# Lead of weight sums, order of block products and deferred token sums in the FFN of a four-layer decoder

## The chip, the cores and the metric

The kernel runs on one core of a Trainium2 chip. The metric is the device time of one execution, in microseconds (us); three runs of the kernel before took 2438.58 to 2440.51 us, median 2439.3. TensorE (PE) multiplies, VectorE (DVE), ScalarE (ACT) and GpSimd (POOL) work element by element, SyncE (SP) issues DMAs. POOL issues DMAs too, and only through its queue are the accumulating ones issued.

## The reference

512 tokens of width 1024 go through four layers in float32. Each layer adds a token mixer (0 and 3: gated linear recurrence "lru"; 1: sparse attention "nsa"; 2: gated linear attention "gla") and then a SwiGLU channel mixer (FFN) of inner width 2816; a last norm follows.

```python
def swiglu(h, w_gate, w_up, w_down):
    return (jax.nn.silu(h @ w_gate) * (h @ w_up)) @ w_down
...
        h = h + y
        h = h + swiglu(rmsnorm(h, ffn_norm[layer]), ffn_w_gate[layer], ffn_w_up[layer], ffn_w_down[layer])
    return rmsnorm(h, final_norm)
```

## The kernel before

**Precision.** Every float32 operand is split into a high part (`hi`, an ACT copy to the short float type) and a low part (`lo`, a DVE subtraction); a product is three matmuls, hi by hi, hi by lo and lo by hi.

**The FFN** of a layer runs in three thirds (8, 8 and 6 tiles of 128 of the inner width), each in two units (4 and 4, 4 and 4, 3 and 3 tiles) and a down projection (`project`, tiles `pj`). So a layer has six units, and the first one directly follows the mixer's output projection. A unit (L551 on) computes gate and up together for its tiles by seven block products in place of eight: `b11`, `t1`, `b22`, `t2`, `t3`, `b21`, `t4`. Each is a `step` (L528): two token halves, four k tiles, three matmuls, so 24 matmuls of 128 columns of tokens by 512 (or 384) of weights. The operands are sums: on the token side a11, a12, a22 and s1 to s4, on the weight side the blocks of gate (b11, b21) and up (b12, b22) for the first and second half of the width, and their sums `t1` = b12+b11, `t2` = b12+b11+b22, `t3` = b12+b22 and `t4` = b12+b11+b22+b21. Steps add up in the PSUM banks X, Z and Y; ACT and DVE copy and combine these between steps (`a`, `z` and the others), so X can hold several products one after another.

**Token sums.** `project` adds each finished bank to h (L494) and calls `finalize` (L423) for it, this calls `combine` (L400): for k under 4 it makes a11 (`ph`, `pl`) and s3; for k from 4 on it makes, in one go, `xf` (h times gain), s1 and s2 (tile `s`, halves `sh`, `sl`), the parts of x (`xh`, `xl`: a12 and a22) and s4. Then `finalize` adds the square (`sq`) for the norm. `norm_sum` (L448), some matmuls `nsum`, a DVE row `ms` and a POOL row `rstd`, comes three steps after the unit's start (`later(3)`).

**Weights.** All weights lie in `wall`, blocks of 512 KB. `uses` (L157) makes one list of them in the order in which PE takes them, with how each is made: plain (one load by SP, L236, into `raws`, tiles `wr`), first (load and one accumulating DMA on POOL's queue, L238, into `big`, tiles `wc`), sum (the same in `raws`), on (an accumulating DMA, L263, onto a tile that was used and split already: `t2` onto the tile of `t1`, `t4` onto that of `t2`). `take` (L270) is called as a step takes its weights: it keeps splits three uses ahead (ACT L258, DVE L259, into a ring of four `ws` tiles), loads five ahead, and in the FFN eight ahead. A load and its adds are issued together.

**What sets the order.** Within an engine rows are queued in the order of the program, as the scheduler of the framework has laid them out; a row that waits holds all rows behind it. So on POOL's queue an add that waits for its load holds later adds and POOL's own arithmetic. The engines run against each other by semaphores.

```python
        tt(s[:, a], x1[:, b], x[:, b], op=OP.subtract)
        tt(s[:, b], s[:, a], x1[:, a], op=OP.subtract)
        sh, sl = self.slot("sh", F32R), self.slot("sl", F32R)
        parts(s, sh, sl)
```

Of the kernel before, what the change touches and what calls it, by code (L numbers as in the profile page):

```python
# [8 lines left out]
F32 = mybir.dt.float32  # L9
F32R = mybir.dt.float32r  # L10
# [174 lines left out]
class Kernel:  # L185
    def __init__(self, tc, ctx, wall, xT, prm, cst, hot, relb, nsm, gsm, out, phases):
# [9 lines left out]
        self.lead.tile([128, pad // 4], F32, name="lead")  # L196
        self.raws = pool("raws", bufs=5)
# [3 lines left out]
        self.slots = pool("slots", bufs=56)  # L201
# [4 lines left out]
        self.raw, self.w = {}, {}  # L206
        self.now = 0
# [14 lines left out]

    RAW_AHEAD, SUM_AHEAD, SPLIT_AHEAD = 5, 8, 3

    def prefetch(self, upto):
        while self.n_dma < min(upto, len(self.uses)):
            i = self.n_dma
            how, blocks = self.uses[i][1:]
            self.n_dma += 1
            if how == "on":  # L230
                continue
            if how == "first":
                r = self.large([128, 1152], "wc")[:, 0:1024]
            else:
                r = self.raws.tile([128, 1024], F32, name=self.name("wr"), tag="wr")
            self.nc.sync.dma_start(r, self.wall[blocks[0]])  # L236
            for b in blocks[1:]:
                self.nc.gpsimd.dma_start(r, self.wall[b], accum_op=OP.add)  # L238
            self.raw[i] = r
# [138 lines left out]
    def new_norm(self, idx):  # L378
# [4 lines left out]
        if idx % 2:  # L383
            self.op = {n: {} for n in ("a11", "a12", "a22", "s1", "s2", "s3", "s4")}

    def gain(self, k):
        return self.prm[:, C_GAIN + self.gidx * 8 + k:C_GAIN + self.gidx * 8 + k + 1]

    def combine(self, k):
# [26 lines left out]
        xh, xl = self.slot("xh", F32R), self.slot("xl", F32R)  # L416
        parts(x, xh, xl)
        if k % 2 == 0:
            self.s4 = self.slot("s4h", F32R), self.slot("s4l", F32R)
        half = (a, b)[k % 2]  # L420
        tt(x[:, a], x[:, a], s[:, b], op=OP.add)
        parts(x[:, a], self.s4[0][:, half], self.s4[1][:, half])
        self.op["a12"][k], self.op["a22"][k] = (xh[:, a], xl[:, a]), (xh[:, b], xl[:, b])  # L423
        self.op["s1"][k], self.op["s2"][k] = (sh[:, a], sl[:, a]), (sh[:, b], sl[:, b])
        self.op["s4"][k] = self.s4[0][:, half], self.s4[1][:, half]

    def finalize(self, k, tk=slice(0, 512)):
# [8 lines left out]
        sq = self.slot("sq")  # L436
        nc.scalar.activation(sq[:, tk], h, AF.Square)
# [89 lines left out]

    def step(self, what, unit, banks, first, last):  # L528
# [17 lines left out]
    def unit(self, l, f, nf, waiting):  # L546
# [9 lines left out]
        for i in self.step("b11", u, X, True, False):
            copy(a1[i], X[i])
        while waiting:
            waiting.pop(0)()
        Z = [self.bank("Z") for _ in range(2)]  # L560
        for i in self.step("t1", u, Z, True, False):
            copy(z1[i], Z[i])
        for i in self.step("b22", u, Z, False, True):
            pass
        for i in self.step("t2", u, X, False, False):
            copy(a2[i], X[i])
            tt(a2[i], Z[i][:, 0:n], a2[i], op=OP.subtract)
        for i in self.step("t3", u, X, False, False):
            tt(z1[i], z1[i], X[i][:, 0:n], op=OP.subtract)
        Y = [self.bank("Y") for _ in range(2)]  # L570
        for i in self.step("b21", u, Y, True, True):
            tt(a1[i], Y[i][:, 0:n], a1[i], op=OP.add)
            silu(a1[i], a1[i], i)
            stt(a2[i], a2[i], self.rstd[:, i:i + 1], a1[i], op0=OP.mult, op1=OP.mult)
# [822 lines left out]
```

## Time and profile before

| | |
|---|---|
| median of three runs | 2439.3 us |
| profiled execution | 2447.19 us |
| its span | 2445.5 us |
| mean granted TensorE clock | 0.975 |
| PE busy | 2327.0 us, 95% |
| DVE / ACT / POOL busy | 60% / 50% / 17% |
| DMA queue q1 (SP) | 250.66 MB, 30.3% of 16 engines |
| DMA queue q0 (POOL) | 100.68 MB, 23.4% of 16 engines |

The span is what the trace covers; the execution's own time is a little longer. A timeline row gives start, duration, engine, line, operation, output and inputs, and in brackets how long the engine had idled just before and what ended that. [...]

### The profile page before, as it was taken

Reading aid. Unit: us, or ns where it says so; the run is one execution under the profiler, and the core shown is the slowest. Engines: PE = TensorE matmul, PEld = TensorE weight load, DVE = VectorE, ACT = ScalarE, POOL = GpSimd, SP = SyncE. Lnnn points to the kernel's source line nnn. Section 1 sums busy time; section 2 is a strip of 40 time slices with the busy share of each in tenths; the row PEclk is TensorE's granted clock in tenths of the full one; section 3 lists DMA queues with packets and bytes.
Section 4 is the critical chain, followed back from the end, with each engine's and each line's share of the span. In section 5 each row is a group of like instructions: output and inputs, shape, how many; then the busy total and the mean of one; then the engine's idle time right before and its main releaser. Section 6 shows DMA issues by size and latency. Waiting matters only on the chain.

```text
span 2445.5 us, 29511 instructions
## 1 busy us (share of the span) xinstructions
PE 2327.0 (95%) x10898; PEld 1941.3 (79%) x10898; DVE 1469.7 (60%) x2388; ACT 1224.6 (50%) x1963; POOL 418.3 (17%) x445
## 2 busy tenths in 40 slices
PE   8997999999999999999989998999989998899998
PEld 7876787887786777887978886788888877788787
DVE  7775546456269987555456536545455886555545
ACT  5954535343368766444445335535344774434344
POOL 1411101001157531010100000101010230101010
PEclk9998999999999999999999998999999999899999
DMA  7235858673421136676862214768684324668682
GB/s 249 86 101 124 207 146 218 157 193 91 143 81 27 44 87 161 184 185 185 207 180 97 82 61 112 183 163 208 170 232 139 104 71 131 152 172 190 175 195 87
DMA packets 102912, 353.21 MB, mean 144 GB/s; under 512 B 11632, under 2 KB 18416, under 8 KB 102768
## 3 DMA queue, kind: packets, MB, share of 16 engines
q1 hardware_dynamic: 75120, 250.66, 30.3%
q0 software_dynamic: 27648, 100.68, 23.4%
q8 instruction: 85, 1.39, 0.2%
q14 instruction: 59, 0.48, 0.1%
HBM read 346.04 MB, written 5.24 MB: 144 GB/s over the span
## 4 chain that ended last, share of the span: by engine, by line
PE 73%; DMA 9%; DVE 8%; ACT 6%; issue 2%; POOL 1%; POOLq 0%; SPq 0%; ACTq 0%; DVEq 0%
PE pj L301 9%; PE pj L302 9%; PE pj L300 9%; DMA wc<-wall 5%; PE X L541 5%; PE X L540 5%; PE X L542 5%; DMA wr<-wall 3%; PE Z L540 2%; PE Z L542 2%; PE Z L541 2%; PE lp L302 2%; PE lp L300 2%; PE lp L301 2%; DVE ws L259 2%
## 5 line engine op out<-in xcount | busy, mean ns | idle before, releaser
L259 DVE TENSOR_TENSOR ws<-wr,ws 128x1024 fp32r<-128x1024 f32 (+1 forms) x402 | 475.5, 1186 | 453.8 <-ACT ws L258 446.4
L258 ACT ACTIVATE ws<-wr 128x1024 fp32r<-128x1024 f32 (+1 forms) x402 | 408.4, 1020 | 466.6 <-PE pj L302 180.7
L259 DVE TENSOR_TENSOR ws<-wc,ws 128x1024 fp32r<-128x1024 f32 (+1 forms) x144 | 163.5, 1135 | 234.4 <-ACT ws L258 233.6
L258 ACT ACTIVATE ws<-wc 128x1024 fp32r<-128x1024 f32 (+1 forms) x144 | 142.2, 988 | 281.5 <-DMA wc<-wall 95.1
L301 PE MATMUL pj<-al,ws 128*128 128x512 f32 (+1 forms) x728 | 278.7, 383 | 0.0
L300 PE MATMUL pj<-ah,ws 128*128 128x512 f32 (+1 forms) x728 | 278.7, 384 | 0.0
L302 PE MATMUL pj<-ah,ws 128*128 128x512 f32 (+1 forms) x728 | 278.4, 382 | 0.0
L238 POOL DMA_DIRECT2D wr<-wall x48 | 42.0, 874 | 696.1 <-DMA wr<-wall 583.2
L263 POOL DMA_DIRECT2D wc<-wall x96 | 87.6, 998 | 421.4 <-DVE ws L259 394.9
L301 PEld LDWEIGHTS pj<-al,ws 128*128 128x128 f32 x728 | 136.9, 188 | 27.1 <-DVE al L329 1.1
L302 PEld LDWEIGHTS pj<-ah,ws 128*128 128x128 f32 x728 | 136.8, 188 | 26.4
L300 PEld LDWEIGHTS pj<-ah,ws 128*128 128x128 f32 x728 | 136.8, 188 | 26.2
L542 PE MATMUL X<-ws,pl 128*128 128x512 f32 (+1 forms) x384 | 142.5, 371 | 0.0
L540 PE MATMUL X<-ws,ph 128*128 128x512 f32 (+1 forms) x384 | 142.4, 371 | 0.0
L541 PE MATMUL X<-ws,ph 128*128 128x512 f32 (+1 forms) x384 | 142.4, 371 | 0.0
L302 PE MATMUL lp<-xh,ws 128*128 128x512 f32 x320 | 126.8, 398 | 10.0 <-DVE ws L259 10.0
L300 PE MATMUL lp<-xh,ws 128*128 128x512 f32 x320 | 127.2, 398 | 6.8 <-ACT ws L258 6.8
L301 PE MATMUL lp<-xl,ws 128*128 128x512 f32 x320 | 126.5, 395 | 0.0
L540 PE MATMUL Z<-ws,sh 128*128 128x512 f32 (+1 forms) x192 | 78.5, 409 | 35.9 <-ACT sh L396 35.9
L540 PE MATMUL Z<-ws,s4h 128*128 128x512 f32 (+1 forms) x192 | 79.4, 414 | 34.5 <-ACT z L552 34.5
L986 POOL TENSOR_TENSOR L<-L,sw 128x512 f32<-128x512 f32 (+3 forms) x128 | 90.9, 750 | 70.8 <-DVE lc L977 25.2
L494 DVE TENSOR_TENSOR h<-h,pj 128x512 f32<-128x512 f32 x116 | 77.5, 684 | 36.1 <-PE pj L302 36.1
(375 smaller groups left out, 5551.6 us busy)
## 6 DMA issues: line engine op xcount, KB each, us to landing
wr<-wall SPq DMA_DIRECT2D x410, 512.0 KB, 4.4
wc<-wall POOLq DMA_DIRECT2D x144, 512.0 KB, 6.8
wc<-wall SPq DMA_DIRECT2D x48, 512.0 KB, 4.3
wr<-wall POOLq DMA_DIRECT2D x48, 512.0 KB, 6.4
scr<-rb SPq DMA_DIRECT2D x16, 192.0 KB, 1.9
h<-xT SPq DMA_DIRECT2D x8, 256.0 KB, 5.7
bias<-scr SPq DMA_DIRECT2D x16, 128.0 KB, 2.7
out<-hg SPq DMA_DIRECT2D x16, 128.0 KB, 1.8
```

Source lines behind the costliest of these rows:

```text
L238: self.nc.gpsimd.dma_start(r, self.wall[b], accum_op=OP.add)
L258: self.nc.scalar.activation(hi, r, AF.Copy)
L259: self.nc.vector.tensor_tensor(lo, r, hi.bitcast(F32), op=OP.subtract)
L263: self.nc.gpsimd.dma_start(whole, self.wall[self.uses[on][2][0]], accum_op=OP.add)
L300: mm(ps, lhsT=wh, rhs=x[0], start=first, stop=False)
L301: mm(ps, lhsT=wh, rhs=x[1], start=False, stop=False)
L302: mm(ps, lhsT=wl, rhs=x[0], start=False, stop=last)
L494: nc.vector.tensor_tensor(self.h[m + c], self.h[m + c], banks[c], op=OP.add)
L540: mm(o, lhsT=xh, rhs=wh, start=first and k == 0, stop=False, skip_group_check=True)
L541: mm(o, lhsT=xh, rhs=wl, start=False, stop=False, skip_group_check=True)
L542: mm(o, lhsT=xl, rhs=wh, start=False, stop=k == 3, skip_group_check=True)
L986: nc.gpsimd.tensor_tensor(p, p, ww.to_broadcast([128, 128 * (i + 1)]), op=OP.mult)
```

## The change

Three things change. (1) The first unit of each FFN (f = 0) takes its products in the order b11, t3, t1, t2, b22, b21, t4 and its `t2` weights are a sum of their own (three blocks in a tile of their own); all other units take t1, b11, b22, t2, t3, b21, t4. (2) Loads and adds are issued apart: sums (first and sum) are loaded up to ten uses ahead, added up to seven; `raws` has six tiles for five, `slots` 54 for 56. (3) `combine` makes s1 at once and puts s2, s4, the parts of x and the squares off to the steps b11, t3, t1 and t2; `norm_sum` runs at the first unit's t2.

```diff
+def unit_order(key):
+    if key[2] == 0:
+        return "b11", "t3", "t1", "t2", "b22", "b21", "t4"
+    return "t1", "b11", "b22", "t2", "t3", "b21", "t4"
...
+                           "t2": ("first", ("b12", "b11", "b22")) if key[2] == 0 else ("on", ("b22",)),
...
-    RAW_AHEAD, SUM_AHEAD, SPLIT_AHEAD = 5, 8, 3
+    RAW_AHEAD, SUM_AHEAD, ADD_AHEAD, SPLIT_AHEAD = 5, 10, 7, 3
+
+    def load(self, i):
+        if i in self.raw or self.uses[i][1] == "on":
+            return
+        how, blocks = self.uses[i][1:]
+        if how == "first":
+            r = self.large([128, 1152], "wc")[:, 0:1024]
+        else:
+            r = self.raws.tile([128, 1024], F32, name=self.name("wr"), tag="wr")
+        self.nc.sync.dma_start(r, self.wall[blocks[0]])
+        self.raw[i] = r
+        if blocks[1:]:
+            self.adds[i] = blocks[1:]
+
+    def add(self, i):
+        for b in self.adds.pop(i, ()):
+            self.nc.gpsimd.dma_start(self.raw[i], self.wall[b], accum_op=OP.add)
...
+    def ahead(self, i):
+
+        self.prefetch(i + self.RAW_AHEAD)
+        for j in range(self.n_dma, min(i + self.SUM_AHEAD, len(self.uses))):
+            if self.uses[j][1] in ("first", "sum"):
+                self.load(j)
+        for j in range(i, min(i + self.ADD_AHEAD, len(self.uses))):
+            self.add(j)
...
             self.prefetch(i + 1)
+            self.add(i)
...
-        self.prefetch(i + 1 + self.RAW_AHEAD)
-        while self.n_dma < min(i + 1 + self.SUM_AHEAD, len(self.uses)) and self.keys[self.n_dma][0][0] in "bt":
-            self.prefetch(self.n_dma + 1)
+        self.ahead(i + 1)
...
         tt(s[:, a], x1[:, b], x[:, b], op=OP.subtract)
-        tt(s[:, b], s[:, a], x1[:, a], op=OP.subtract)
-        sh, sl = self.slot("sh", F32R), self.slot("sl", F32R)
-        parts(s, sh, sl)
...
+        parts(s[:, a], sh[:, a], sl[:, a])
...
+        def second():
+            tt(s[:, b], s[:, a], x1[:, a], op=OP.subtract)
+            parts(s[:, b], sh[:, b], sl[:, b])
...
+        for n, f in (("s2", second), ("s4", fourth), ("x", plain)):
+            self.waits[n].append(f)
...
+        for f in self.waits.pop({"b11": "s2", "t3": "s4", "t1": "x", "t2": "sq"}.get(what), ()):
+            f()
+        if what == "t2" and unit[1] == 0:
+            self.norm_sum()
...
+            elif what == "t2" and first:
+                tt(a2[i], a2[i], X[i][:, 0:n], op=OP.subtract)
+                tt(z1[i], z1[i], X[i][:, 0:n], op=OP.subtract)
...
+            elif what == "t3" and first:
+                tt(a2[i], X[i][:, 0:n], a1[i], op=OP.subtract)
...
+            elif what == "b22" and first:
+                tt(a2[i], Z[i][:, 0:n], a2[i], op=OP.add)
...
-        self.later(3, self.norm_sum)
```

The counts: PE has as many matmuls as before; DVE has 27 rows more, ACT some 8 more, SP 8 loads more and POOL 8 adds more over the kernel. Three places of the queues follow; line numbers of the changed kernel are its own, and banks are named there after the step that opens them (`b11` is the former X, `t1` the former Z).

PE in the first unit of layer 0, before: the last of `b11` has run, and `t1` (Z) begins; `ws_299` is the first of its two weight tiles, `sh` and `sl` its token sums.

```order
L540 MATMUL Z_346_1769<-ws_299_1583,sh_302_1605 128x512
L541 MATMUL Z_346_1769<-ws_299_1583,sh_302_1605 128x512
L542 MATMUL Z_346_1769<-ws_299_1583,sl_303_1606 128x512
L540 MATMUL Z_347_1770<-ws_299_1583,sh_302_1605 128x512
L541 MATMUL Z_347_1770<-ws_299_1583,sh_302_1605 128x512
L542 MATMUL Z_347_1770<-ws_299_1583,sl_303_1606 128x512
L540 MATMUL Z_346_1769<-ws_299_1583,sh_311_1639 128x512
L541 MATMUL Z_346_1769<-ws_299_1583,sh_311_1639 128x512
L540 MATMUL Z_347_1770<-ws_299_1583,sh_311_1639 128x512
L541 MATMUL Z_347_1770<-ws_299_1583,sh_311_1639 128x512
```

The same place after the change, from `b11`'s last row on; `ws_329` and `ws_334` are the two `t1` weight tiles.

```order
L586 MATMUL b11_327_1688<-ws_300_1585,pl_285_1477 128x512
L584 MATMUL t1_337_1786<-ws_329_1706,sh_304_1610 128x512
L584 MATMUL t1_338_1787<-ws_329_1706,sh_304_1610 128x512
L585 MATMUL t1_337_1786<-ws_329_1706,sh_304_1610 128x512
L586 MATMUL t1_337_1786<-ws_329_1706,sl_305_1611 128x512
L584 MATMUL t1_337_1786<-ws_329_1706,sh_308_1631 128x512
L585 MATMUL t1_337_1786<-ws_329_1706,sh_308_1631 128x512
L586 MATMUL t1_337_1786<-ws_329_1706,sl_309_1632 128x512
L584 MATMUL t1_337_1786<-ws_334_1751,sh_312_1652 128x512
L585 MATMUL t1_338_1787<-ws_329_1706,sh_304_1610 128x512
```

And a few rows on, still in the first unit after the change, where `t1`'s last rows with `ws_334` meet the first of `t3` (`ws_301`, onto the bank of `b11`, with the `ph` of k below 4).

```order
L584 MATMUL t1_337_1786<-ws_334_1751,sh_316_1673 128x512
L585 MATMUL t1_337_1786<-ws_334_1751,sh_316_1673 128x512
L586 MATMUL t1_337_1786<-ws_334_1751,sl_317_1674 128x512
L584 MATMUL b11_326_1687<-ws_301_1589,ph_269_1435 128x512
L585 MATMUL b11_326_1687<-ws_301_1589,ph_269_1435 128x512
L586 MATMUL b11_326_1687<-ws_301_1589,pl_270_1436 128x512
```

`t1` still comes first on PE, though the program has `t3` ahead of it; 21 of its 24 rows stand before `t3`, and the halves alternate in another way.

POOL's queue from the first to the second unit of layer 0, before: L238 is the add issued beside a load, L263 the add onto a used tile (`wc_362` and `wc_364`, the second unit's `t1`, twice: for `t2`, then for `t4`).

```order
L455 TENSOR_TENSOR rstd_356_1846<-ms_355_1844,mhalf_91 128x4
L238 DMA wr_384_2015<-wall 128x1024
L238 DMA wc_446_2411<-wall 128x1024
L238 DMA wc_448_2441<-wall 128x1024
L238 DMA wr_386_2021<-wall 128x1024
L263 DMA wc_362_1889<-wall 128x1024
L263 DMA wc_364_1895<-wall 128x1024
L263 DMA wc_362_1889<-wall 128x1024
L263 DMA wc_364_1895<-wall 128x1024
L238 DMA wc_486_2753<-wall 128x1024
```

After the change: L247 is the add beside or behind a load, L287 the add onto a used tile; `wc_349` and `wc_352` are the second unit's `t1`, `wr_372` and `wr_375` its `t3`, `wc_297` and `wc_299` the first unit's `t2`.

```order
L287 DMA wc_299_1558<-wall 128x1024
L247 DMA wr_372_1983<-wall 128x1024
L247 DMA wr_375_1990<-wall 128x1024
L495 TENSOR_TENSOR rstd_359_1864<-ms_358_1862,mhalf_91 128x4
L247 DMA wc_422_2287<-wall 128x1024
L247 DMA wc_425_2294<-wall 128x1024
L287 DMA wc_349_1810<-wall 128x1024
L287 DMA wc_352_1817<-wall 128x1024
L287 DMA wc_349_1810<-wall 128x1024
L287 DMA wc_352_1817<-wall 128x1024
```

The second unit's `t3` adds stood among the `wc` adds, directly ahead of `t2`'s; now they stand ahead of `rstd`, before both adds of the following third's first sums.

POOL's queue in the NSA mixer, before: scalings of the attention weights `L`, then the low parts of the keys (`kl`).

```order
L986 TENSOR_TENSOR L_912_5347<-L_912_5347,sw_951_5474 128x128 x4
L901 TENSOR_TENSOR kl_938_5439<-kw_821_4897,kh_937_5438 64x512
L902 TENSOR_TENSOR kl_938_5439<-kw_821_4897,kh_937_5438 64x512
L912 TENSOR_TENSOR qq_958_5505<-qw_763_4621,qq_958_5505 64x512
L912 TENSOR_TENSOR qq_959_5508<-qw_763_4621,qq_959_5508 64x512
```

After the change:

```order
L1046 TENSOR_TENSOR L_914_5363<-L_914_5363,sw_953_5490 128x128 x4
L247 DMA wr_1389_7010<-wall 128x1024
L961 TENSOR_TENSOR kl_940_5455<-kw_823_4913,kh_939_5454 64x512
L962 TENSOR_TENSOR kl_940_5455<-kw_823_4913,kh_939_5454 64x512
L972 TENSOR_TENSOR qq_960_5521<-qw_765_4637,qq_960_5521 64x512
L972 TENSOR_TENSOR qq_961_5524<-qw_765_4637,qq_961_5524 64x512
```

The add of a `t3` sum of the following FFN now stands between the scalings and `kl`.

## Rows read from the trace of the kernel before

**Rows 1.** The page, busy time by engine: busy us, share of the span, instructions.

```profile
PE 2327.0 (95%) x10898; PEld 1941.3 (79%) x10898; DVE 1469.7 (60%) x2388; ACT 1224.6 (50%) x1963; POOL 418.3 (17%) x445
```

**Rows 2.** Waits of PE by what it waited for: us in total, times, longest us.

```profile
PE Z L540 <- ACT sh L396: 35.9, 12, 4.8
PE Z L540 <- ACT z L552: 34.5, 12, 7.4
```

**Rows 3.** Windows over two stretches of 192 gate/up matmuls without a wait (a unit and the first step of the next), tiles of 512 and of 384 columns. The columns: window, its length, busy us of PE, weight loads, DVE, ACT and POOL (with instructions), granted clock, DMA share, GB/s.

```profile
345.90:389.43 43.53, 43.53 (x194) 35.99 (x192) 25.73 (x28) 23.50 (x27) 5.28 (x7) 1.00 0.78 197
471.50:504.77 33.27, 33.27 (x193) 33.24 (x192) 20.22 (x27) 18.80 (x27) 4.17 (x6) 1.00 0.76 199
```

**Rows 4.** Windows over the first unit of each FFN, layers 0 to 3, from the first matmul of `b11` to the end of `t4`; columns as in rows 3.

```profile
195.20:253.77 58.57, 46.08 (x177) 35.98 (x176) 36.85 (x54) 31.22 (x44) 6.26 (x7) 0.83 0.51 120
918.60:968.03 49.43, 43.33 (x177) 33.78 (x176) 35.02 (x51) 30.16 (x43) 6.48 (x6) 0.93 0.62 144
1501.26:1559.36 58.10, 45.61 (x177) 35.62 (x176) 37.03 (x54) 30.16 (x43) 6.33 (x7) 0.82 0.56 131
2060.08:2120.90 60.82, 48.33 (x177) 37.72 (x176) 36.86 (x54) 31.21 (x44) 6.26 (x7) 0.80 0.47 116
```

**Rows 5.** Timeline of PE in the first unit of layer 0: one of the waits in `t1`, two matmuls after it, and the matmuls of the norm.

```profile
211.97 0.80 PE L540 MATMUL Z<-ws,sh 128*128 128x512 f32 x1 [4.80 <-ACT sh L396]
...
212.99 0.63 PE L542 MATMUL Z<-ws,sl 128*128 128x512 f32 x1
213.42 0.63 PE L540 MATMUL Z<-ws,sh 128*128 128x512 f32 x1
...
223.34 0.83 PE L451 MATMUL nsum<-ones,sq 128*128 128x1 f32 x6
```

**Rows 6.** Timeline of ACT at the start of the same unit.

```profile
194.04 1.06 ACT L258 ACTIVATE ws<-wc 128x1024 fp32r<-128x1024 f32 x1 [8.46 <-PE pj L302]
195.00 0.70 ACT L400 ACTIVATE xf<-h,prm 128x512 f32<-128x512 f32 x1
...
197.66 0.64 ACT L396 ACTIVATE sh<-s 128x512 fp32r<-128x512 f32 x1 [1.00 <-DVE s L413]
...
216.24 0.63 ACT L396 ACTIVATE sh<-s 128x512 fp32r<-128x512 f32 x1 [0.95 <-DVE s L413]
```

**Rows 7.** Windows over the second unit of the thirds with 4 and 4 tiles, eight in all, from the first matmul of `t1` to the first of the down projection: two of them, and the sum of the eight. Columns as in rows 3.

```profile
391.09:426.17 35.08, 33.04 (x147) 27.04 (x146) 21.23 (x25) 17.74 (x22) 4.36 (x6) 1.00 0.87 215
...
2255.04:2290.05 35.01, 33.31 (x148) 26.96 (x146) 21.15 (x25) 17.74 (x22) 3.91 (x5) 1.00 0.87 214
sum 285.16, PE 270.83 PEld 219.87 DVE 169.67 ACT 142.05 POOL 31.72; mean PE 33.85 PEld 27.48 DVE 21.21 ACT 17.76 POOL 3.96
```

**Rows 8.** The same for the second units of the thirds with 3 and 3 tiles, layers 0 to 3.

```profile
506.00:535.61 29.61, 25.91 (x147) 25.03 (x146) 17.16 (x23) 14.43 (x22) 2.44 (x3) 1.00 0.83 203
1215.81:1250.34 34.53, 27.59 (x148) 27.27 (x147) 17.34 (x23) 14.66 (x22) 6.32 (x9) 0.90 0.89 227
1805.26:1840.52 35.26, 27.88 (x147) 27.55 (x146) 17.34 (x23) 14.65 (x22) 4.24 (x6) 0.85 0.87 221
2369.88:2399.07 29.19, 25.90 (x148) 25.00 (x146) 17.16 (x23) 14.43 (x22) 1.84 (x3) 1.00 0.81 206
```

**Rows 9.** Timelines of POOL (three rows), ACT (two) and PE (one) around the second unit of layer 0.

```profile
245.54 0.92 POOL L238 DMA_DIRECT2D wr<-wall  x1 [19.62 <-DMA wr<-wall]
...
260.06 0.86 POOL L238 DMA_DIRECT2D wr<-wall  x1 [4.37 <-DMA wr<-wall]
260.60 2.11 POOL L263 DMA_DIRECT2D wc<-wall  x2
...
272.29 1.06 ACT L258 ACTIVATE ws<-wc 128x1024 fp32r<-128x1024 f32 x1 [7.79 <-DMA wc<-wall]
273.25 0.58 ACT L552 ACTIVATE z<-Z 128x512 f32<-128x512 f32 x1
...
273.89 0.79 PE L540 MATMUL Z<-ws,s4h 128*128 128x512 f32 x1 [4.58 <-ACT z L552]
```

**Rows 10.** The page, groups of instructions: line, engine, operation, tiles, count, busy us, mean ns of one, idle before.

```profile
L259 DVE TENSOR_TENSOR ws<-wc,ws 128x1024 fp32r<-128x1024 f32 (+1 forms) x144 | 163.5, 1135 | 234.4 <-ACT ws L258 233.6
```

**Rows 11.** The page, DMA queues (packets, MB, share of 16 engines over the span), and DMA issues (count, KB each, median us from issue to landing).

```profile
q1 hardware_dynamic: 75120, 250.66, 30.3%
q0 software_dynamic: 27648, 100.68, 23.4%
...
wr<-wall SPq DMA_DIRECT2D x410, 512.0 KB, 4.4
wc<-wall POOLq DMA_DIRECT2D x144, 512.0 KB, 6.8
```

**Rows 12.** Windows in layer 2 ahead of the second unit of three tiles: the middle of the projection before that third, and the end of the third's first unit. Columns as in rows 3.

```profile
1745.00:1770.00 25.00, 25.00 (x112) 20.71 (x111) 9.07 (x11) 3.61 (x4) 2.60 (x3) 1.00 0.55 131
1788.00:1805.00 17.00, 17.00 (x103) 16.96 (x102) 12.41 (x18) 10.19 (x16) 3.91 (x6) 1.00 0.94 286
```

**Rows 13.** Timelines of SP (one row) and POOL (two) in the NSA mixer.

```profile
722.30 0.33 SPq L236 DMA_DIRECT2D wr<-wall  x1
...
723.69 1.28 POOL L901 TENSOR_TENSOR kl<-kw,kh 64x512 fp32r<-64x512 f32 x1
...
753.09 1.04 POOL L986 TENSOR_TENSOR L<-L,sw 128x512 f32<-128x512 f32 x1 [6.04 <-DVE lc L977]
```

More of the change, by code (lines that the diff above doesn't have):

```diff
@@ L170, in uses @@
         wall = lambda b, k: at[(b,) + unit + (k,)]
-        for step, how, blocks in (("b11", "plain", ("b11",)), ("t1", "first", ("b12", "b11")), ("b22", "plain", ("b22",)),
-                                  ("t2", "on", ("b22",)), ("t3", "sum", ("b12", "b22")), ("b21", "plain", ("b21",)),
-                                  ("t4", "on", ("b21",))):
+        for step in unit_order(key):
+            how, blocks = {"b11": ("plain", ("b11",)), "t1": ("first", ("b12", "b11")), "b22": ("plain", ("b22",)),
+                           "t2": ("first", ("b12", "b11", "b22")) if key[2] == 0 else ("on", ("b22",)),
+                           "t3": ("sum", ("b12", "b22")), "b21": ("plain", ("b21",)), "t4": ("on", ("b21",))}[step]
             for k in (0, 2):
@@ L205, in __init__ @@
         self.pos = self.n_dma = self.n_split = 0
-        self.raw, self.w = {}, {}
+        self.raw, self.w, self.adds = {}, {}, {}
         self.now = 0
@@ L227, in prefetch @@
             i = self.n_dma
-            how, blocks = self.uses[i][1:]
             self.n_dma += 1
[L230 to L239, printed above, removed]
+            self.load(i)
+    def ahead(self, i):
[5 more added lines that the diff above has]
+            self.add(j)
     def split_ahead(self, upto):
@@ L384, in new_norm @@
             self.op = {n: {} for n in ("a11", "a12", "a22", "s1", "s2", "s3", "s4")}
+            self.waits = {n: [] for n in ("s2", "s4", "x", "sq")}
     def gain(self, k):
@@ L430, in finalize @@
             self.combine(k)
+            if k >= 4:
+                self.waits["sq"].append(lambda: self.square(k, tk))
+                return
         elif self.gidx < 8:
@@ L435, in finalize @@
             self.x[k] = (hi, lo)
[L436 to L437 removed]
+        self.square(k, tk)
         if self.gidx == 8:
@@ L526, in last, with step @@
         end(1)
-    def step(self, what, unit, banks, first, last):
+    def step(self, what, unit, banks, first):
         mm = self.nc.tensor.matmul
         n = unit[2] * 128
+        for f in self.waits.pop({"b11": "s2", "t3": "s4", "t1": "x", "t2": "sq"}.get(what), ()):
+            f()
+        if what == "t2" and unit[1] == 0:
+            self.norm_sum()
         ws = [self.take((what,) + unit[:2] + (k,), 2) for k in (0, 2)]
@@ L553, in unit @@
         silu = lambda o, src, t: nc.scalar.activation(o, src, AF.Silu, scale=self.rstd[:, t:t + 1])
-        X = [self.bank("X") for _ in range(2)]
+        X, Y, Z = [], [], []
         a1, z1, a2, sg = two("a1"), two("z1"), two("a2"), two("sg")
[L556 to L574, printed above, removed]
@@ L575, in unit, with after @@
-        for i in self.step("t4", u, X, False, True):
-            silu(sg[i], X[i][:, 0:n], 2 + i)
-            stt(z1[i], z1[i], self.rstd[:, 2 + i:3 + i], sg[i], op0=OP.mult, op1=OP.mult)
+        first = f == 0
+        order = unit_order((None, l, f))
+        def after(what, i):
+            if what == "b11":
+                copy(a1[i], X[i])
+            elif what == "t1":
+                copy(z1[i], Z[i])
+            elif what == "t2" and first:
+                tt(a2[i], a2[i], X[i][:, 0:n], op=OP.subtract)
+                tt(z1[i], z1[i], X[i][:, 0:n], op=OP.subtract)
+            elif what == "t2":
+                copy(a2[i], X[i])
+                tt(a2[i], Z[i][:, 0:n], a2[i], op=OP.subtract)
+            elif what == "t3" and first:
+                tt(a2[i], X[i][:, 0:n], a1[i], op=OP.subtract)
+            elif what == "t3":
+                tt(z1[i], z1[i], X[i][:, 0:n], op=OP.subtract)
+            elif what == "b22" and first:
+                tt(a2[i], Z[i][:, 0:n], a2[i], op=OP.add)
+            elif what == "b21":
+                tt(a1[i], Y[i][:, 0:n], a1[i], op=OP.add)
+                silu(a1[i], a1[i], i)
+                stt(a2[i], a2[i], self.rstd[:, i:i + 1], a1[i], op0=OP.mult, op1=OP.mult)
+            elif what == "t4":
+                silu(sg[i], X[i][:, 0:n], 2 + i)
+                stt(z1[i], z1[i], self.rstd[:, 2 + i:3 + i], sg[i], op0=OP.mult, op1=OP.mult)
@@ L578, in unit @@
+        into = {"b11": X, "t2": X, "t3": X, "t4": X, "t1": Z, "b22": Z, "b21": Y}
+        for at, what in enumerate(order):
+            banks = into[what]
+            new = not banks
+            if new:
+                banks += [self.bank(what) for _ in range(2)]
+            for i in self.step(what, u, banks, new):
+                after(what, i)
+            if at == 0:
+                while waiting:
+                    waiting.pop(0)()
         return a2 + z1
```

29 lines of the change are left out of this document (18 added, 11 removed).

## The prediction

> **What bounds the kernel now.** I read the busy row first: TensorE (PE) is busy 2327.0 of 2445.5 us [rows 1], so at most some 118 us of idling can be had, and whatever half clock lies inside the busy time. Next the waits by engine: nearly all of PE's lost time hangs on two tiles, 35.9 us on `sh` and 34.5 us on `z`, twelve times each [rows 2]. Then windows laid on the stages where these tiles are used. A stretch of 192 gate/up matmuls without a wait takes 43.53 us at granted clock 1.00, 0.2267 us for each; in the short third 33.27, 0.1733 each [rows 3]. Against these two yardsticks I hold two kinds of stretch.
>
> First, the four FFN entries, the first unit after each mixer: 58.57, 49.43, 58.10 and 60.82 us, sum 226.92, at granted clocks of 0.80 to 0.93 [rows 4]. 168 matmuls by 0.2267 are 38.09, and with about 1.1 for the norm's small matmuls (0.83 for six, [rows 5]) 39.2. So 226.92 − 4 × 39.2 = 70.1 us are lost there. Why is to be seen on ScalarE (ACT): its split of the `t1` weights waits 8.46 us for the projection (the ring of split weights is full), the scaling of h4 stands right behind it, and from there the four `sh` come one whole chain of `combine` apart, the first at 197.66, the last at 216.24 [rows 6], some 6.2 us for each of three. [...]
>
> Second, the second unit of each third, from the start of `t1` to the down projection: eight of four tiles sum to 285.16 us [rows 7]. The clean rate gives 144 × 0.2267 = 32.65 each, so 24.0 are lost. Four of three tiles take 29.61, 34.53, 35.26 and 29.19, sum 128.59 [rows 8]; 144 × 0.1733 = 24.95 each, so 28.8 are lost. Together 52.8. The first shows the cause: the `t3` add of this unit reaches the head of POOL's queue and waits 4.37 us for its own load, to 260.06; only then the adds that make `t2` of `t1` go out at 260.60; ACT waits 7.79 us for that tile to 272.29, and the copy of Z behind it releases PE at 273.89 [rows 9].
>
> **The change part by part.**
>
> *Entry: order and split of the token sums.* The matmul count stays. In the new unit `t1` no longer waits for one long chain per k: `s1` alone (256 columns) is made at once, while `s2`, `s4`, `x` and the squares move behind it. On PE's list, though, most of `t1` still stands ahead of `t3`, so `t3` doesn't cover the `s1` chain; what helps is the shorter chain. I step the new lists of ACT, DVE and PE from the same start, 195.20. ACT splits `t3`'s weights at 194.04, as it did `t1`'s, then h4 at 195.00 and h5 two microseconds later (a scaling takes 0.70, a 256-wide copy less than the 0.64 of a 512-wide, [rows 6]). The `t1` weights now stand third in the ring and wait for `b11`'s buffers: its 18th matmul ends at 195.20 + 18 × 0.2267 = 199.3, the ACT half takes 1.06 [rows 6], the DVE half 1.14 [rows 10], so waits of about 0.3 and 0.75 at the first `t1` weight, 0.45 and 0.2 at the second, which needs `b11`'s end at 200.6: 1.7 in all. Then `t3` and `t2` run without a wait. Before `b22` the copies of Z stand on ACT behind a split (1.06) that needs a buffer of `t2`, and a copy is 0.58 [rows 9]: 1.65. That makes 39.2 + 1.7 + 1.65 = 42.5, and I add 1 us for a clock that is granted late: 43.5 for layers 0, 2 and 3. In layer 1 the split before `b22` waits for earlier matmuls, and 39.2 plus 1.5 make 40.7. Entries: 226.9 − 3 × 43.5 − 40.7 = **−55.7**. The ends: no wait at all, 226.9 − 156.8, −70; the half clock stays as it is, rival B, −32.
>
> The added DVE work (`a2` and `z1` less X, `a2` plus Z: some seven rows in each entry, one ACT copy less) is costed at nothing: a row of 512 columns is half a split's 1.14 [rows 10], 4 us in all. DVE is busy 36.85 in the 58.57 us of the entry [rows 4], and 41 would fit into 43.5 by little; but the `b11` and `t1` splits of the next unit, some 4.5 us of it, now fall behind `b21`. If this cover is gone, it costs at most the 4 us by which DVE grows, in each entry. `norm_sum` later in the unit costs nothing as long as rstd comes before `b21`'s silu; by the new POOL list two `t3` adds stand ahead of it, done by about 223 in my stepping, rstd by 229, the silu at 232.
>
> The half clock is the larger part of what an entry loses. After the 4.80 wait the spacing is 0.43 [rows 5], yet a second unit that lost 2.4 us (391.09, 35.08 against 32.65) shows 1.00 [rows 7]. The waits that I expect are of the second size. [...]
>
> *Second units: loads and adds with leads of their own.* The `t3` sums are loaded up to ten uses ahead and added up to seven, so they no longer stand in POOL's queue unready ahead of the `t2` adds; and `b11` now lies between `t1` and `t2`, one more step, 24 × 0.2267 = 5.44 us, to land in. An add lands in 6.8 us at the median [rows 11]. For eight units of four tiles this covers the 4.58 that PE waited [rows 9], and I leave 0.5 each: 4. For the four of three tiles the DMA engines set a floor. In layer 2 they worked 0.87 × 35.26 = 30.7 us in it, layer 1 0.89 × 34.53 = 30.7, both above the 24.95 of PE; layers 0 and 3 24.6 and 23.6 [rows 8]. The busiest stretch I found has a share of 0.94 [rows 12]. If nothing starts sooner, 30.7 / 0.94 is 32.7, 7.7 over; in layers 0 and 3 26.2 and 25.1, 1.4 over together. But one project stage ahead the share is only 0.55, 25 × 0.39 = 9.8 us of room [rows 12], and two uses more of lead are 2 loads and 2 adds. Their price: queue q1 moves 250.66 MB in 30.3% of the span, 2.96 us a MB, q0 100.68 in 23.4%, 5.68 [rows 11]; 0.524 MB is 1.55 for a load, 2.98 for an add, 9.1 for two of each. So the rest lies between 0 and 7.7 for each of layers 1 and 2; I take half, 4. Left: 4 + 1.4 + 8 = 13.4. Second units: 13.4 − 52.8 = **−39.4**; ends −53 and 0.
>
> *The full sums of `t2`.* Eight loads and eight adds more, 2 × 1.55 + 2 × 2.98 = 9.1 us of DMA for each FFN, lie in the entry, where the DMA share is 0.47 to 0.62 [rows 4]: at nothing. If they push loads of the second unit out instead, that is rival C.
>
> *Waits that are new.* On POOL the add of an early `t3` sum now stands in the NSA mixer ahead of `kl`, which ran at 723.69. Its load can't go out before a raw buffer is read; there, SP's load goes at 722.30 [rows 13], a load takes 4.4 [rows 11], so the add is held to 726.7, 3.0 us and 0.86 for its issue. Behind it wait `kl`, `qq` and the scalings of L, and PE's products after them; POOL next idles 6.04 us at 753.09 [rows 13]. Ends: 0 (that idle swallows it) and 19.6, the longest wait of POOL for a load that I saw [rows 9]. I take **+4**, by the row itself.
>
> **Sum.** −55.7 − 39.4 + 4 = −91.1. The profiled execution took 2447.2 us (span 2445.5), so 2356.1 by it. The median of the runs, 2439.3, lies 7.9 lower: **2348 us**.
>
> **Rivals.**
>
> B: the entry stays at half clock. The waits are shorter, but four follow each other, with `t1` still ahead of `t3`. Its price is the busy time beyond 39.2: 46.08, 43.33, 45.61 and 48.33 [rows 4] make 6.9 + 4.1 + 6.4 + 9.1 = 26.5, of which 3 are in my sum: 2348 + 23.5 = 2372. (Then the entries give only the idle part, 70.1 − 26.5 = 43.6, less the new waits of 11.6: 32.) For: clocks of 0.80 to 0.83 in three layers. Against: 0.93 in layer 1 [rows 4], and 1.00 in a unit with 2.4 us of waits [rows 7].
>
> C: the DMA engines bound the units. Nothing is gained in the second units, since the bytes don't shrink and 16 transfers are added. For: shares of 0.81 to 0.89 there [rows 7, 8]. Against: 0.55 just ahead [rows 12], and POOL's 4.37 of plain queueing [rows 9]. 2348 + 39.4 = 2388. [...]
>
> D: the entries aren't cured, because ACT and DVE need as long for `s1` with four splits between as for the old chain: 2348 + 55.7 = 2404. Against: the stepping above.
>
> E: slower. POOL's queue is held at the entry: rstd stands behind two `t3` adds that wait for their loads. The add at 245.54 waited 19.62 so [rows 9]; if rstd comes at 246 rather than 229, the silu of `b21` is 14 us late, X and Y stay full and PE stops, in four layers 57 us; and the adds of the second units, in the same queue, are late with it, as in C. 2348 + 57 + 39.4 = 2444. With C it decides from 51.7 / 4 = 13 us of late silu on, rstd at 245, 50 us after the entry's start; without C from 91.1 / 4 = 23, 60 us after it. For: POOL has no second queue for its DMAs. Against: those loads go out with the longer lead, and the raw ring has a sixth buffer.
>
> **How the numbers follow.** Forecast 0.57, B 0.18, C 0.12, D 0.05, E 0.04, and 0.04 for better than the forecast by more than 28 us (every loss gone: 2447.2 − 70 − 53 − 7.9 = 2316). The range from 2320 to 2396 leaves out D, E and the best. A measurement of this kernel can tell 0.2%, about 5 us: faster 0.95, within it 0.01, slower 0.04.
>
> **What would show it.** Right: PE's waits on `sh` and `z` fall from 70 us to under 20; the four entries take 40 to 45 us at clocks above 0.95; the eight second units of four tiles take 33 to 34; POOL no longer stands before its `t3` add in a second unit. Wrong: entries over 50 us; a granted clock under 0.9 there; DMA shares above 0.9 over whole units with ACT waiting on `wc`; rstd later than `b21`; PE waiting on POOL in the NSA mixer for more than 10 us.

## The result, and the profile after

The changed kernel takes 2360.8 us (median of four runs, 2358.75 to 2364.9) against 2439.9 before (2438.58 to 2441.1, measured beside it): ratio 0.9678, 95% interval 0.9661 to 0.9695, 3.2% faster. The forecast was 2348, with 2320 to 2396 as the range: right side, inside the range, 12.6 us too low. The profiled executions fell from 2447.19 to 2358.75, by 88.4 us; the sum by their own time was 91.1.

Busy time after; [rows 1] has the same line of before. PE's idle time fell from 118 to 54 us:

```profile
PE 2302.9 (98%) x10898; PEld 1927.3 (82%) x10898; DVE 1474.8 (63%) x2420; ACT 1221.8 (52%) x1971; POOL 424.9 (18%) x453
```

The waits of PE after (us in total, times, longest). The two lines of [rows 2], 70.4 us together, are gone. `z` is left with 5.6; `b` and `t` are the renamed banks; the `lp` lines belong to the kernel's start and were there before:

```profile
PE lp L324 <- DVE ws L283: 10.0, 2, 5.0
PE lp L322 <- ACT ws L282: 6.8, 1, 6.8
PE t L584 <- ACT z L596: 5.6, 4, 1.8
PE b L584 <- ACT ws L282: 5.4, 4, 1.8
```

The four entries after, windows as in [rows 4]. Their sum fell from 226.92 to 173.26 us:

```profile
193.99:237.13 43.14, 40.60 (x177) 31.82 (x176) 37.89 (x61) 29.98 (x46) 8.88 (x11) 1.00 0.79 200
889.50:930.31 40.81, 40.01 (x177) 32.04 (x176) 35.59 (x57) 28.40 (x43) 7.39 (x8) 1.00 0.79 195
1457.79:1502.43 44.64, 42.11 (x177) 33.03 (x176) 38.25 (x62) 29.01 (x45) 8.57 (x11) 0.96 0.77 191
1998.00:2042.67 44.67, 42.14 (x177) 33.03 (x176) 37.98 (x61) 29.97 (x46) 9.06 (x11) 0.96 0.80 201
```

The second units after: the last six steps before the down projection, 144 matmuls, as in [rows 7, 8] (they begin with `b11` now). First the sum of the eight of four tiles, then the four of three tiles:

```profile
sum 262.35, PE 262.20 PEld 216.87 DVE 170.50 ACT 143.74 POOL 27.63; mean PE 32.78 PEld 27.11 DVE 21.31 ACT 17.97 POOL 3.45
```

```profile
480.05:505.10 25.05, 25.05 (x147) 25.05 (x145) 17.34 (x23) 14.67 (x22) 1.72 (x2) 1.00 0.70 211
1173.66:1206.87 33.21, 30.00 (x147) 28.40 (x146) 17.28 (x23) 14.42 (x22) 4.38 (x6) 0.85 0.93 234
1745.34:1777.60 32.26, 28.43 (x147) 27.13 (x146) 17.25 (x23) 14.42 (x22) 3.29 (x5) 0.89 0.96 245
2285.57:2310.63 25.06, 25.06 (x147) 25.06 (x146) 17.34 (x23) 14.68 (x22) 1.73 (x2) 1.00 0.65 197
```

The units of four tiles and two of three run at the clean rate, within 0.6 us; layers 1 and 2 keep 8 and 7 us of loss in their last second unit. That loss isn't idle time alone: PE idles 3.2 and 3.8 us in them, and is busy 5.0 and 3.4 us longer than the 25.05 of the clean ones, at granted clocks of 0.85 and 0.89. In all 413.75 went to 262.35 + 115.58 = 377.93. Entries −53.7 and second units −35.8 make −89.5; the span fell by 88.4, so the rest of the kernel is 1.1 us longer.

### The profile page after: what moved, and what is told of

Its sections match the earlier page's. It is cut to its first block, busy times and chain, and to the rows that moved or that the text cites. A ratio compares the mean times of both kernels' runs of the same rounds, so it can differ in the third digit from the quotient of the medians.

```text
span 2357.1 us, 29570 instructions
## 1 busy us (share of the span) xinstructions
PE 2302.9 (98%) x10898; PEld 1927.3 (82%) x10898; DVE 1474.8 (63%) x2420; ACT 1221.8 (52%) x1971; POOL 424.9 (18%) x453
## 4 chain that ended last, share of the span: by engine, by line
PE 82%; DVE 8%; ACT 5%; DMA 3%; issue 1%; POOL 1%; POOLq 0%; SPq 0%; DVEq 0%; ACTq 0%
PE pj L323 9%; PE pj L324 9%; PE pj L322 9%; PE b L585 7%; PE b L586 7%; PE b L584 7%; DMA wc<-wall 3%; PE t L585 3%; PE t L586 3%; PE t L584 3%; PE lp L324 2%; PE lp L322 2%; PE lp L323 2%; DVE ws L283 2%; PE at L650 1%
## 5 line engine op out<-in xcount | busy, mean ns | idle before, releaser
L287 POOL DMA_DIRECT2D wc<-wall x88 | 79.7, 962 | 434.6 <-DVE ws L283 422.6
L584 PE MATMUL b<-ws,ph 128*128 128x512 f32 (+1 forms) x384 | 143.5, 374 | 0.0
L585 PE MATMUL b<-ws,ph 128*128 128x512 f32 (+1 forms) x384 | 142.4, 371 | 0.0
L586 PE MATMUL b<-ws,pl 128*128 128x512 f32 (+1 forms) x384 | 142.4, 371 | 0.0
L586 PE MATMUL b<-ws,xl 128*128 128x512 f32 (+1 forms) x384 | 142.4, 371 | 0.0
L247 POOL DMA_DIRECT2D wc<-wall x64 | 58.2, 910 | 466.8 <-DMA wc<-wall 183.9
L584 PE MATMUL b<-ws,xh 128*128 128x512 f32 (+1 forms) x384 | 142.4, 372 | 0.0
L585 PE MATMUL b<-ws,xh 128*128 128x512 f32 (+1 forms) x384 | 142.4, 371 | 0.0
L247 POOL DMA_DIRECT2D wr<-wall x48 | 41.6, 867 | 427.8 <-DMA wr<-wall 213.8
```

Of the source, the lines that this page charges most:

```text
L247: self.nc.gpsimd.dma_start(self.raw[i], self.wall[b], accum_op=OP.add)
L287: self.nc.gpsimd.dma_start(whole, self.wall[self.uses[on][2][0]], accum_op=OP.add)
L584: mm(o, lhsT=xh, rhs=wh, start=first and k == 0, stop=False, skip_group_check=True)
L585: mm(o, lhsT=xh, rhs=wl, start=False, stop=False, skip_group_check=True)
L586: mm(o, lhsT=xl, rhs=wh, start=False, stop=k == 3, skip_group_check=True)
```

## The experiments

Each kernel's row sums the same windows over its own trace, that is over one execution, which can lie some us off the median (2447.19 against 2439.9 for the kernel before, 2352.72 against 2359.0 for e11); "median" is over four runs. The kernel before had medians of 2442 to 2444 beside e1 to e11, 2 to 4 us more than beside the changed kernel, which was not timed again; differences of that size between an experiment and 2360.8 show nothing.

| run | entries | second units | median us |
|---|---|---|---|
| before | 226.9 | 413.8 | 2439.9 |
| after | 173.3 | 377.9 | 2360.8 |
| e1 leads, sums nearly at once | 202.9 | 379.4 | 2393.3 |
| e2 split sums alone | 161.9 | 412.5 | 2384.5 |
| e3 order and leads | 199.5 | 376.1 | 2384.4 |
| e4 new order in first units only | 171.7 | 377.1 | 2359.7 |
| e5 old order, split sums, leads | 161.8 | 380.3 | 2350.6 |
| e6 after, next sums late | 171.7 | 363.4 | 2341.3 |
| e7 after, five raw buffers | 171.7 | 378.8 | 2357.9 |
| e8 before, six raw buffers | 228.6 | 382.8 | 2419.2 |
| e9 e5, next sums late | 161.7 | 362.2 | 2331.6 |
| e10 after, next adds late | 173.3 | 363.0 | 2338.9 |
| e11 after, t1 before t3 | 169.1 | 371.8 | 2359.0 |

### e1 to e4: which part carries which term

e1 gives every unit the old order and lets `combine` do all at once:

```diff
-    if key[2] == 0:
-        return "b11", "t3", "t1", "t2", "b22", "b21", "t4"
-    return "t1", "b11", "b22", "t2", "t3", "b21", "t4"
+    return "b11", "t1", "b22", "t2", "t3", "b21", "t4"
...
-            self.waits[n].append(f)
+            f()
```

> Only the separate leads of loads and adds (and the sixth raw buffer) are kept; every unit has the order of before and combine makes all token sums at once. Theory S (the split token sums cure the entries, the leads cure the second units): the entries stay at about 227 us in sum with some 36 us of waits on sh, the twelve second units lose about 16 us instead of 53, so 2400 to 2410 us. Theory O (the order of the products carries both gains, the leads are only what makes it possible): second units still lose 40 or more, 2430 to 2440 us.

2393.3 us, below both ranges. The second units are cured (379.4) but for the two in layers 1 and 2, so it isn't the order that cures them. The entries fell as well, to 202.9: in this edit s1 and s2 are still split apart, 256 columns each, so `sh` of s1 no longer waits for s2. PE waits 2.55 us three times in layer 0's entry, where it had waited up to 4.80 [rows 5].

e2 keeps only the split of `combine`: the order is that of e1's diff, loads, adds and buffers are those of before, and the deferred parts run at steps that fit the old order:

```diff
-        for f in self.waits.pop({"b11": "s2", "t3": "s4", "t1": "x", "t2": "sq"}.get(what), ()):
+        for f in self.waits.pop({"b11": "s2", "t1": "s4", "b22": "x", "t2": "sq"}.get(what), ()):
```

> Only the split of combine is kept: s1 at once, s2 at b11, s4 at t1, x at b22, squares at t2; order, leads and buffers as before. Theory S: the entries fall to 43 to 47 us each (173 to 188 in sum) and the second units still lose 53 us: 2385 to 2402 us. Theory O: t1 still comes right behind b11, its waits stay, entries over 215 in sum, 2425 to 2440 us.

2384.5 us: theory S, with entries still shorter than it said: 161.9, 11 us less than in the changed kernel. The second units are as before.

e3 has the change's order and leads, and `combine` at once (the second half of e1's diff).

> The changed kernel with combine making all token sums at once, as before (order and leads of the change kept). Theory S: t3 can hide one step of 5.4 us of the chain, no more, so the entries take 50 to 55 us each and the time is 2385 to 2405 us, the second units being cured. Theory O: the entries are cured by the order too, 43 to 46 each, 2358 to 2370 us.

2384.4 us: the entries are 199.5, next to e1's 202.9, nearer to theory S. With all sums made at once, the order gives them 3 us.

e4 gives all but the first units the old order.

> The changed kernel with the old order (b11, t1, b22, t2, t3, b21, t4) in all units but the first of each FFN. Theory S: the leads alone carry the second units; 2358 to 2370 us, t2 lands in time without b11 between. Theory O: without b11 between t1 and t2 the second units lose 30 us or more again, 2385 to 2400 us.

2359.7 us, no different from after: `b11` between `t1` and `t2` isn't needed.

### e5: without the new order

The order of e1's diff and the map of e2's; leads and six buffers stay; `t2` comes from `t1`'s tile again. No run has the old order with `t2` sums of their own, so a cost of the new order, here and below, includes theirs.

> The changed kernel with the old order in every unit, the first ones too, and t2 made on t1's tile again (8 loads and 8 adds fewer); split token sums (s4 at t1, x at b22) and the leads kept. Theory P (the new order of the first unit costs time, the split sums alone cure the entries): the entries fall from 173 to 162 to 166 us in sum, second units stay near 378: 2344 to 2353 us. Theory Q (the entries of the run with split sums alone were short because the old leads left POOL and the DMA engines free): the entries stay at 171 to 176, 2357 to 2365 us.

2350.6 us, ratio 0.9623 (0.9595 to 0.9650): theory P. PE's one wait above 0.3 us in layer 0's entry is this (the entry is 40.50 us):

```profile
205.46 0.50 PE L582 MATMUL t<-ws,sh 128*128 128x512 f32 x1 [0.88 <-ACT sh L417]
```

where the changed kernel has these two (43.14):

```profile
200.94 0.50 PE L585 MATMUL t<-ws,sh 128*128 128x512 f32 x1 [0.53 <-DVE ws L283]
...
219.58 0.50 PE L584 MATMUL t<-ws,s4h 128*128 128x512 f32 x1 [1.79 <-ACT z L596]
```

### e6 and e10: the two units that stayed slow

e6 writes one column of each tile of the next FFN's first sums from h before the load, so that loads and adds can't start while the FFN before still runs:

```diff
+        if how == "first" and self.uses[i][0][2] == 0 and self.uses[i][0][1] > 0:
+            self.nc.scalar.activation(r[:, 0:1], self.h[0][:, 0:1], AF.Copy)
         self.nc.sync.dma_start(r, self.wall[blocks[0]])
```

> The changed kernel, with one small ACT copy from h into each tile of the next FFN's first weight sums before its load, so that these loads and adds can't start before the end of the FFN before. Theory T (in layers 1 and 2 the last second unit of three tiles waits because the next layer's sums, 2 loads and 2 adds, share the DMA engines and POOL's queue with its t2 adds): those two units fall from 33.2 and 32.3 us to 25 to 27, the DMA share in them under 0.8, 2345 to 2353 us. Theory U (the unit's own bytes set the pace there): both stay over 31, 2358 to 2366 us.

2341.3 us, a little below the range: both units at 25.05, with DMA shares of 0.72 and 0.71, theory T. e10 leaves the loads where they are and holds back the adds alone:

```diff
+        if i in self.adds and self.uses[i][1] == "first" and self.uses[i][0][2] == 0 and self.uses[i][0][1] > 0:
+            self.nc.vector.scalar_tensor_tensor(self.raw[i][:, 0:1], self.h[0][:, 0:1], 0.0, self.raw[i][:, 0:1], op0=OP.mult, op1=OP.add)
         for b in self.adds.pop(i, ()):
```

> The changed kernel; of the next FFN's first sums only the adds are held back (one tiny DVE row on the tile that needs h, times zero), their loads stand in SP's queue as before. Theory Q (head of line: the add that waits for its load holds the ready t2 adds in POOL's queue): the last second units of layers 1 and 2 fall from 33.2 and 32.3 to 25 to 27 us, 2340 to 2350 us. Theory T2 (the load's share of the DMA engines does it as much): both stay over 29, 2354 to 2362 us.

2338.9 us, a little below Q's range, and both units at 25.07 and 25.06: holding back the adds alone is enough. (Of the 21.9 us to the changed kernel 15.0 lie in the second units and 5.3 in the NSA mixer, for which see the last section.) The place in layer 2, after: SP loads the next layer's two sums, POOL's add on the first of them stands ahead of the two `t2` adds (L287), and these go out at 1742.38:

```profile
1732.65 1.66 SPq L240 DMA_DIRECT2D wc<-wall  x2
...
1741.84 0.86 POOL L247 DMA_DIRECT2D wc<-wall  x1 [7.67 <-DVE z L626]
1742.38 2.11 POOL L287 DMA_DIRECT2D wc<-wall  x2
...
1754.37 0.84 ACT L282 ACTIVATE ws<-wc 128x768 fp32r<-128x768 f32 x1 [6.16 <-DMA wc<-wall]
...
1755.27 0.44 PE L584 MATMUL b<-ws,sh 128*128 128x384 f32 x1 [1.34 <-ACT ws L282]
```

`t1`'s tile had been split by ACT at 1735.03. The profile puts the end of POOL's 7.67 us down to a DVE row that ended at about that time, but the two loads took this long to land, the first until about 1741.3:

```profile
DMA to landing us min/median/max: 8.6/9.0/9.4
```

At the same place in layer 1 of e5 (where L245 and L285 are the two kinds of add) the profile names the loads:

```profile
1167.36 0.86 POOL L245 DMA_DIRECT2D wc<-wall  x1 [8.18 <-DMA wc<-wall]
1169.24 0.86 POOL L245 DMA_DIRECT2D wc<-wall  x1 [1.02 <-DMA wc<-wall]
1169.78 2.11 POOL L285 DMA_DIRECT2D wc<-wall  x2
```

The same place in e10, with the same loads: ACT splits `t1` at 1722.86, the first `t2` add goes out 2.1 us later, and ACT finds its tile ready:

```profile
1720.49 1.66 SPq L240 DMA_DIRECT2D wc<-wall  x2
...
1722.86 0.83 ACT L284 ACTIVATE ws<-wc 128x768 fp32r<-128x768 f32 x1
...
1724.98 0.86 POOL L289 DMA_DIRECT2D wc<-wall  x1 [2.93 <-DVE ws L285]
...
1736.59 0.85 ACT L284 ACTIVATE ws<-wc 128x768 fp32r<-128x768 f32 x1 [0.55 <-PE b L588]
```

In the changed kernel the first `t2` add went 7.35 us behind the split (1742.38 − 1735.03), so 5.2 us were lost in POOL's queue. The two adds also took longer to land; first the changed kernel, then e10, then e6, where the next layer's loads are away too:

```profile
DMA to landing us min/median/max: 11.9/13.5/15.2
DMA to landing us min/median/max: 9.2/10.7/12.3
DMA to landing us min/median/max: 7.6/8.7/9.8
```

e10 takes the held adds out of the unit with their bytes: its DMA work falls from 0.96 × 32.26 = 31.0 us to 0.92 × 25.06 = 23.1. So by itself it doesn't part their place in the queue from their bytes. Other traces do, in the main: high shares go with a PE at full rate in e10 and close to it in e11, which has the adds in the same order and the same stretch, but where the loads landed sooner (5.8 us for the first) and the first `t2` add went out 4.56 us behind the split (1740.99 − 1736.43). And in e5 and e8 the same kind of unit is slow at lower shares. The rows: e10 and e11 in layer 2, then e5 and e8 in layer 1.

```profile
1733.18:1758.24 25.06, 25.06 (x148) 25.06 (x147) 17.33 (x23) 14.79 (x22) 1.72 (x2) 1.00 0.92 279
1746.75:1773.21 26.46, 25.62 (x148) 25.04 (x146) 15.37 (x21) 13.52 (x22) 2.18 (x3) 1.00 0.99 291
1170.44:1204.40 33.96, 28.18 (x148) 27.86 (x147) 17.44 (x24) 14.67 (x22) 4.92 (x7) 0.90 0.88 219
1199.39:1235.34 35.95, 27.86 (x148) 27.54 (x147) 17.34 (x23) 14.65 (x22) 4.23 (x6) 0.86 0.86 221
```

### e7 and e8: leads or the sixth buffer

e7 is the changed kernel with `bufs=5` for `raws`; e8 is the kernel before with `bufs=6` and 54 slots.

> The changed kernel with five raw buffers in place of six. Theory V (the sixth buffer, which lets both t3 sums be loaded and added ahead of the next sums, is what cures the second units): they lose 30 us or more again, 2385 to 2400 us. Theory L (the separate leads do it, with five buffers too): 2358 to 2368 us.

> The kernel before with six raw buffers (and 54 slots) and nothing else changed. Theory V: the second units lose 25 us or less in place of 53, entries as before, 2405 to 2418 us. Theory L: both terms as before, 2432 to 2442 us.

2357.9 and 2419.2 us, the one at the lower end of theory L's range, the other 1.2 above V's. Neither theory was the whole: second units are 378.8 with the leads and five buffers, and 382.8 with six buffers and no leads at all. Either one puts both `t3` adds ahead of the adds of the following third's first sums in POOL's queue (read in layer 0). e8 also shows that entries don't follow from the buffers (228.6).

### e9: both gains

e5 with e6's edit, under the old order.

> The run with the old order everywhere, split sums and leads, and with it the ACT copy that holds the next FFN's first sums back. If the two effects are separate they add: entries 162 us, all twelve second units at the clean rate (8 by 32.7, 4 by 25.1, sum 362), so 2350.6 less 18: 2330 to 2336 us. If the entries pay for the later sums (their weights arrive too late behind the mixer's own loads), they go over 170: 2340 to 2350 us.

2331.6 us, ratio 0.9547 (0.9527 to 0.9568): 29 us faster than the changed kernel and the fastest of all. The effects add.

### e11: what the new order costs

```diff
-        return "b11", "t3", "t1", "t2", "b22", "b21", "t4"
+        return "b11", "t1", "t3", "t2", "b22", "b21", "t4"
```

> The changed kernel with b11, t1, t3, t2, b22, b21, t4 in the first unit, so that ACT and DVE split the weights in the order in which PE already takes them. Theory M (the first unit of the change loses its 2.3 us of waits because weights of t3 are split ahead of those of t1, and the copies of z stand behind a later split): entries 162 to 167 us in sum, 2349 to 2356 us. Theory N (the loss lies at b22, with t2's own sum and the deferred sums in front): entries stay at 171 to 175, 2357 to 2363 us.

2359.0 us, entries 169.1 in its trace: neither theory. In layer 0's entry the wait on `ws` is gone and the one at `b22` is 0.45, but one of 2.19 on the last `sh` has come. ACT's rows in e11 show why: a weight split that waits for `t1`'s matmuls stands ahead of h7's scaling (L423), and `sh` behind that.

```profile
203.96 1.06 ACT L282 ACTIVATE ws<-wc 128x1024 fp32r<-128x1024 f32 x1 [0.79 <-PE t L586]
204.93 0.70 ACT L423 ACTIVATE xf<-h,prm 128x512 f32<-128x512 f32 x1
206.70 0.42 ACT L419 ACTIVATE sh<-s 128x256 fp32r<-128x256 f32 x1 [1.07 <-DVE s L436]
```

In e5 the scaling stands ahead of that split:

```profile
202.84 0.71 ACT L421 ACTIVATE xf<-h,prm 128x512 f32<-128x512 f32 x1
203.74 1.06 ACT L280 ACTIVATE ws<-wc 128x1024 fp32r<-128x1024 f32 x1 [0.20 <-ACT xf L421]
204.99 0.42 ACT L417 ACTIVATE sh<-s 128x256 fp32r<-128x256 f32 x1 [0.19 <-DVE s L434]
```

So the place of single rows in ACT's queue decides a wait of 1 to 2 us. Whether another layout with `t3` ahead would be as good as the old order stays open.

## Why the prediction was right, and where it was wrong

**Entries: right in size.** 173.3 against the 171.2 stepped out; 43.14 for layer 0 against 43.5, 40.81 for layer 1 against 40.7. The wait at `b22` was put at 1.65 and was 1.79, for the reason given, copies of Z on ACT behind a split:

```profile
218.00 1.04 ACT L282 ACTIVATE ws<-wr 128x1024 fp32r<-128x1024 f32 x1
218.95 1.06 ACT L596 ACTIVATE z<-t 128x512 f32<-128x512 f32 x2
```

Of the four waits in `t1`, 1.7 us in all, only one above 0.3 showed, 0.53. The 1 us for the clock didn't come as a lower clock in layer 0 (1.00), but PE is busy 40.60 there, 1.4 over the 39.2 of the yardstick, for a cause that stays open. The 1.5 us by which layers 2 and 3 are longer came with a granted clock of 0.96. The text named the shorter chain as what helps, and e2 and e5 show that. What it didn't see is that the new order, with its own `t2` sums, costs: split sums with the old order take 161.8, 11.5 us less, of which 5.2 are idle time of PE and 6.3 busy time. The old order has hardly any of the waits that the term allows for. The sixteen more transfers are hidden, as costed: in none of the four entries does ACT, which splits the weights, wait for a DMA, and e5, without them, has the same second units within 2.4 us.

**Second units: −39.4 put, −35.8 measured.** For the four-tile units 4 us were left over; they keep 262.35 − 8 × 32.65 = 1.2. For those of three tiles in layers 0 and 3 1.4 was put and 0.2 found. The step that failed is "the DMA engines set a floor" for layers 1 and 2: 4 us each were put, 8.3 and 7.3 remain. These lie next to the 7.7 of the floor's own sum, and the shares of 0.93 and 0.96 with ACT waiting 6.16 us on `wc` are a sign that the text gave for being wrong; yet e11 runs such a unit at 26.46 and e5 and e8 are slow at shares of 0.86 to 0.88. The DMA work in those windows held the next layer's sums, which the unit doesn't need (with them away e6 has 0.71 × 25.05 = 17.8 us), and their adds stood ahead of the `t2` adds in POOL's queue. That is the very mechanism that the text names for the other units, at a place where it wasn't looked for.

**The NSA term, +4.** The add that was to hold `kl` wasn't held: it went out at 693.01 behind the scalings, without idle time, and `kl` followed at once:

```profile
693.01 0.85 POOL L247 DMA_DIRECT2D wr<-wall  x1
693.94 1.27 POOL L961 TENSOR_TENSOR kl<-kw,kh 64x512 fp32r<-64x512 f32 x1
```

The step that failed is the one that took its load for the one that SP issues at 722.30 before [rows 13]; here the load had landed. The mixer's stretch is 1.5 us longer all the same (348.60 to 350.10), with PE busy 2.1 us longer at a clock of 0.99 for 1.00, and not idle for longer.

**The offset, −7.9.** This is the larger part of the miss. By the profiled time, 2356.1 was forecast and 2358.75 came: 2.7 too low. The 7.9 us by which the profile of before lay above its median were carried over; the profile of after lies 2.0 below its own. 2.7 + 7.9 + 2.0 = 12.6. The offset is one execution's, not the kernel's. That the terms together are only 2.7 off is in part luck: the gains in entries and second units were put 2.0 and 3.6 us too high, and the loss in the NSA mixer 2.5 too high.

**The rivals.** B didn't happen: the clock is 1.00, 1.00, 0.96 and 0.96 in the entries. That several short waits in a row would hold the entry at half rate was the author's estimate. The kernel before shows 0.50 in the window from 212.90 to 220.00, behind the wait of 4.80; here the entries with waits of 0.53 and 1.79 run at 0.96 to 1.00. C looked true of two units, and e10 and e11 took it away: the transfers fit. With the loads beside them in e10 the two `t2` adds took 9.2 and 12.3 us to land, in e6 without these loads 7.6 and 9.8, and the unit ran clean in both, at 25.06 and 25.05. D fell with the entries, E too: rstd came 33.0 us after the entry's start (227.00 − 193.99), well ahead of the 50 at which it would decide:

```profile
224.42 0.86 POOL L247 DMA_DIRECT2D wr<-wall  x1 [1.86 <-DVE sq L485]
227.00 1.04 POOL L495 TENSOR_TENSOR rstd<-ms,mhalf 128x4 f32<-128x4 f32 x1 [1.72 <-DVE ms L493]
```

## What to carry to other kernels

When a queue issues DMAs that wait for data, read which rows stand ahead of the one that the tensor engine needs: in layer 2 an unready add held two ready ones for 4 to 5 us; two units with such a hold took 7 to 8 us longer, in part at a lower clock (0.85 and 0.89), whereas a DMA share of 0.92 went with no loss (25.06 us). Where one change has several parts, take each away once: here the split of a long chain gave all of one term, a sixth buffer or leads of their own for loads and adds would each have given most of the other, and the third part, a new order with its `t2` sums, cost 10 us that didn't show in a total that had improved.

## What was not expected of the hardware

The same wait doesn't always cost the same clock. PE waits 1.79 us before `b22` in layers 0, 2 and 3 of the changed kernel; layer 0 stays at 1.00 and takes 43.14 us, layers 2 and 3 show 0.96 and take 44.64 and 44.67. It isn't the layer: with the same wait layer 2 shows 1.00 in e4 and e6 (43.16 and 43.14 us), and layer 3 in e7 (43.15). In the NSA mixer one wait of some 3.16 us, for a gate, is followed by transposes of 0.45 us each group in the changed kernel and of 0.66 in e4:

```profile
574.92 0.45 PE L867 MATMUL ngt<-ident,gf 48*128 48x48 f32 x4 [3.15 <-ACT gf L861]
```

```profile
576.37 0.66 PE L867 MATMUL ngt<-ident,gf 48*128 48x48 f32 x4 [3.16 <-ACT gf L861]
```

Over the 35 us from its end on e4's granted clock is 0.91, that of the changed kernel 0.95, of e10, with the same wait, 1.00, and the mixer as a whole takes 353.2, 350.1 and 344.8 us in the three. Its own code is the same; the FFN's transfers that stand among its rows are not. Of the 8.4 us between e4 and e10, 5.55 are longer busy time of PE and 2.85 idle time. So several us of difference between two kernels can lie in a stretch whose own code neither edit changes, which is why the table goes by stages.
